# Branch A's output gates finished in the group's head, queries swapped by transfers, residual gate with moving columns, four probability buffers

## Chip, cores and metric

One core of a Trainium2 chip. The metric is the device time of one execution in microseconds (us); lower is better. The engines are named as in the profile: PE (matmul), PEld (its weight loads), DVE, ACT, POOL, and SP, whose queue issues every transfer of this kernel.

## What is computed

One encoder layer over two groups ("prompt", "sample") of 1024 tokens and width 1024, with shared weights, all in float32.

```
mod = silu(c) @ w_ada + b_ada;  shift, scale, gate = split(mod, 3)
h = rms_norm(x, norm_g) * (1 + scale) + shift
qa, ka, va, za, qb, kb, vb, zb, ga, gb = split(h @ w_in)
oa = gqa_attention(rope(rms(qa)), rope(rms(ka)), va) * silu(za)     # 8 query heads of 64, 2 kv heads
ob = rms(diff_attention(rope(rms(qb)), rope(rms(kb)), vb, lam)) * (1 - lam_init) * silu(zb)  # 4 heads, 2 maps
merged = sigmoid(ga) * (oa @ w_proj_a) + sigmoid(gb) * (ob @ w_proj_b)
y = x + gate * (merged @ w_out)
```

## The kernel before

**Precision.** Most products are made of float32r parts: a high part (ACT copies it) and a low part (DVE or POOL subtracts), with three matmuls for a pair of split operands. Weights come in by `load_w` through the tag `st` (3 buffers) and are split at L177 (ACT) and L179 (POOL, or DVE where the engines are alone).

**Stages of a group.** (1) A *head*: keys and values of branch A (`kva_gen`) and half of its queries (`qa_gen`), woven with a few banks of `z_gen`. (2) Six phases of attention, `phase(0)` to `phase(4)` and a last one; in each, attention is woven with filler work on PE: projections still needed (`proj_tt`, L488) and `z_gen` (L667), which makes the gate inputs za, zb, ga, gb. (3) The merge (L940) and the output projection `out_gen` (L969). The second group's normalisation (`ht_gen`) runs beside the first group's output projection.

**z_gen.** There are 12 items of 4 banks; a bank is 24 matmuls of 512 columns. ACT copies a finished bank to the tile `ev` (L673), and a transfer parks it in device memory as `zd`. `Z_HEAD` says how many of the 48 banks go to the head, `Z_SHARE` how many to each phase, and the rest comes in the last phase. Before, `gated_gen` reads a parked bank back in the last phase, applies Silu (L895), and multiplies the attention output by it.

**rms.** Each projected tile of tokens goes through ACT (copy L500, square L501), DVE (sum L504), POOL (L505: scale and epsilon; L506: power −0.5), and a rotation on POOL or DVE (L508 to L528). PE then transposes it (L539), and ACT and DVE split it (L541, L542). In a head, the engine of the rotation alternates by tile, and tile *t* is transposed after tile *t*+2 was projected (`LAG`).

**Attention.** A unit is 256 queries (two tiles of 128) of one head. A query tile holds its high part in one half of the partitions and its low part in the other; scores need it a second time with the halves exchanged. `swapped` makes that copy, `sw`, on POOL (L565), a tile of 128 queries at a time. Scores are four matmuls (L697, L698) into one of two PSUM banks `s`; DVE takes the negated maximum (L699); ACT takes the exponential (L700) into a tile `p` of the pool `ppool` (3 buffers). `flip` then transposes in 32×32 blocks on DVE (L734), and four transfers (L739) put `p` into `q`, from where the values are multiplied (L759, L760 in branch A, L799 in branch B). In branch B there are two maps for each query tile, joined on DVE (L733). A `p` buffer comes free when its transfers have landed.

**Order.** `weave` interleaves the streams by the shares in the tables (`ATT_W`, `IN_A`, `Z_A`, `LAST_ATT`, `LAST_FILL` and so on), attention is emitted at high priority, and a scheduler then sets each engine's order from its own estimate of times. Each engine and SP's queue run their instructions strictly in that order.

**The residual's gate.** `gate_gen` runs once, for both groups, in the first group's last phase. Before, the weights are the stationary operand and the moving one, `cT`, has 2 columns (L435), 64 matmuls that run as 128 instructions.

Of the kernel before, what the change touches and what calls it, by code (L numbers as in the profile page):

```python
# [48 lines left out]
    (0.1, 0.05, 0.45, 0.1, 0.15, 0.55),  # L49
)  # L50
Z_A = (
    (0.15, 0.0, 0.2, -0.1, 0.0, 0.0),
    (0.15, 0.05, 0.35, 0.05, 0.0, -0.1),
)
LAST_ATT, LAST_FILL = (44, 32)
GATED_A = -0.1
TAIL = 6
TAIL_A = 0.3
LAG = 2

# [28 lines left out]
def kernel(ctx: ExitStack, tc: tile.TileContext, t: dict):  # L89
# [336 lines left out]
    def gate_gen():  # L426
        for n in range(NCH):
            ps = gbank()[:, :2]
            for q in range(2):
                st = spool.tile([P, 4, P], F32, tag="st", name=nm("st"))  # L430
                col = 2 * D + n * P
                dma(st, w_ada[q * 512 : (q + 1) * 512, col : col + P].rearrange("(c p) n -> p c n", p=P))
                for c in range(4):
                    k = q * 4 + c
                    nc.tensor.matmul(ps, st[:, c], cT[:, k], start=(k == 0), stop=(k == NCH - 1))  # L435
            nc.vector.tensor_scalar(out=gatec[:, n], in0=ps, scalar1=bcol[:, 2, n : n + 1], scalar2=None, op0=ALU.add)
            yield 1
# [58 lines left out]
    def rms(ps, nh, e):  # L496
        n = nh * HD
        row = rtile()
        raw, sq = row[:, :n], row[:, 256 : 256 + n]
        nc.scalar.activation(raw, ps, AF.Copy)  # L500
        nc.scalar.activation(sq, raw, AF.Square)  # L501
        ss = tiny.tile([P, 4], F32, tag="ss", name=nm("ss"))[:, :nh]
        rs = tiny.tile([P, 4], F32, tag="rs", name=nm("rs"))[:, :nh]
        nc.vector.tensor_reduce(out=ss, in_=sq.rearrange("p (h d) -> p h d", d=HD), axis=AX.X, op=ALU.add)  # L504
        nc.gpsimd.tensor_scalar(out=ss, in0=ss, scalar1=1.0 / HD, scalar2=EPS, op0=ALU.mult, op1=ALU.add)  # L505
# [52 lines left out]
    def swapped(u, qt):  # L558

        qs = u["q"]  # L560
        sw = mtile("sw", [P, 2, P], F32R)[:, : len(qs)]
        sl = slice(qt * P, (qt + 1) * P)
        for m, q in enumerate(qs):
            for a, b in ((LO, HI), (HI, LO)):
                nc.gpsimd.tensor_scalar(  # L565
                    out=sw[a, m], in0=q[b, sl].bitcast(F32), scalar1=1.0, scalar2=1.0, op0=ALU.mult, op1=ALU.mult
                )
        return sw

# [26 lines left out]
    def qa_gen(st, half):  # L596
# [12 lines left out]
        def back(tt, x3):  # L609
            sl = slice(tt * P, (tt + 1) * P)  # L610
            pairs_T(x3, qs[0][:, :, sl], qs[1][:, :, sl])

        yield from pipelined(ht, w, front, back)

    def qkb_gen(ht, out, h):
# [40 lines left out]
    def z_gen(ht, col, dst, i0):  # L656
        w = load_w(w_cols(w_in, (col, 256)))
        for hf in range(2):
            for e in range(2):
# [13 lines left out]
                nc.scalar.activation(ev, ps, AF.Copy)  # L673
# [31 lines left out]
    def scores(u, i):  # L705
# [4 lines left out]
        if m == 0:  # L710
            u["sw"] = u["next"] if "next" in u else swapped(u, qt)
        pt = ptile()
        su = u["su"][:, qt : qt + 1] if m == 0 else tiny.tile([P, 1], F32, tag="su", name=nm("su"))
        softmax_unit(u["q"][m][:, qt * P : (qt + 1) * P], u["sw"][:, m], u["k"][m], pt, su)
        if m == 0:
            u[t] = [pt]
            u.pop("next", None)
# [114 lines left out]
    def attention(units):  # L832
# [3 lines left out]
        for n, (ph, make) in enumerate(units):  # L836
# [7 lines left out]
        for at, ph, n, i, qk in steps:  # L844
# [4 lines left out]
            with tc.high_priority(offset=AHEAD):  # L849
# [12 lines left out]
                if t is not None:  # L862
                    late.append(lambda u=live[n], t=t: flip(u, t))
                    if t == 0:
                        late.append(lambda u=live[n]: u.update(next=swapped(u, u["pr"] * 2 + 1)))
                    elif n + 1 < len(units) and units[n + 1][0] == ph:
                        live[n + 1] = units[n + 1][1]()
                        late.append(lambda u=live[n + 1]: u.update(next=swapped(u, u["pr"] * 2)))
# [5 lines left out]
    def gated_gen(st, i, hf, oT):  # L874
# [15 lines left out]
        for c in range(2):  # L890
# [4 lines left out]
            nc.scalar.activation(z, z, AF.Silu)  # L895
# [109 lines left out]
    def units_of(st):  # L1005
# [17 lines left out]

        units = []
        for half in range(2):
            units += [(half, lambda a=(half, i, pr): a_unit(*a)) for i in (0, 2, 1, 3) for pr in range(4)]
        for h in range(4):
            units += [(2 + h, lambda a=(h, pr): b_unit(*a)) for pr in range(4)]
# [9 lines left out]
    def z_item(st, i):  # L1038
        ht = st["ht"]
        if i < 2:  # L1040
            return z_gen(ht, C_ZA + i * 256, st["zd"], i * 2)
        if i < 4:
            return z_gen(ht, C_ZB + (i - 2) * 256, st["zd"], i * 2)
# [118 lines left out]
```

## Time and profile before

| | |
|---|---|
| runs | 2009.33, 2014.87, 2015.93 us; median 2014.87 |
| the profiled execution | 2017.56 us, span 2015.8 us, mean granted PE clock 0.974 |
| busy share | PE 95%, PEld 82%, DVE 65%, ACT 51%, POOL 48% |
| transfers | 278 MB, all large ones on one queue, 46.2% of the 16 DMA engines' span |

PE is busy nearly throughout, so time can be lost on it in two ways that the share does not show apart: short waits, and stretches in which its clock is granted at half. A window of the trace tells both: its length less PE's busy time, and the column of the granted clock.

### The profile page before, as it was taken

What the parts mean: (1) busy time and instruction counts of PE and PEld (TensorE: products, weight loads), DVE (VectorE), ACT (ScalarE), POOL (GpSimd) and SP (SyncE); (2) the same over time, 40 slices, a digit from 0 to 9 for tenths busy, and PEclk for the clock granted to TensorE, in tenths of its full rate; (3) what the DMA queues carried; (4) which work ended last, traced back from release to release, by engine and by line L of the source; (5) the groups of instructions that cost most, each with busy time, mean ns of one, the idle gap of its engine ahead of it and who ended that gap; (6) DMA issues with size and microseconds to landing.
All of it is one profiled execution on the core that took longest, in us unless ns stands there. A gap on an engine that the chain in (4) does not pass through costs nothing.

```text
span 2015.8 us, 31269 instructions
## 1 busy us (share of the span) xinstructions
PE 1924.6 (95%) x10554; PEld 1650.9 (82%) x10554; DVE 1305.9 (65%) x1798; ACT 1029.6 (51%) x1956; POOL 963.1 (48%) x1640
## 2 busy tenths in 40 slices
PE   8889999999999999889998899999999999998999
PEld 3778888888978988768888787888887888876887
DVE  4557766776787476546464778667777746664741
ACT  4445655565554345754323556566665434587420
POOL 2475723564677471331235675246577837522210
PEclk9999999999999996999998899999999999999999
DMA  8124545555443327754650345464544323565531
GB/s 306 48 71 109 147 139 137 148 150 154 109 125 95 90 81 206 223 191 160 208 188 32 99 123 152 137 169 126 157 127 126 88 74 90 160 212 192 183 119 73
DMA packets 255199, 278.35 MB, mean 138 GB/s; under 512 B 31680, under 2 KB 205888, under 8 KB 255040
## 3 DMA queue, kind: packets, MB, share of 16 engines
q1 hardware_dynamic: 255040, 276.36, 46.2%
q8 instruction: 84, 1.38, 0.3%
q14 instruction: 75, 0.61, 0.1%
HBM read 133.59 MB, written 42.01 MB: 87 GB/s over the span
## 4 chain that ended last, share of the span: by engine, by line
PE 58%; DVE 10%; DMA 10%; POOL 7%; ACT 6%; issue 5%; SPq 3%; ACTq 0%; POOLq 0%; DVEq 0%
PE f L667 15%; PE f L488 14%; PE f L969 4%; PE s L697 4%; PE s L698 4%; PE s L969 3%; DMA q<-p 3%; PE a L799 3%; DMA p<-zd 2%; PE a L759 2%; PE a L760 2%; SPq L739 2%; DVE m L699 2%; PE f L940 2%; ACT p L700 2%
## 5 line engine op out<-in xcount | busy, mean ns | idle before, releaser
L667 PE MATMUL f<-u,w 128*128 128x512 f32 x2208 | 580.6, 399 | 0.0
L488 PE MATMUL f<-w,u 128*128 128x256 f32 x3456 | 492.2, 288 | 2.8 <-ACT row L500 1.6
L488 PEld LDWEIGHTS f<-w,u 128*128 128x128 f32 x3456 | 464.1, 193 | 24.0 <-ACT row L500 2.7
L667 PEld LDWEIGHTS f<-u,w 128*128 128x128 f32 x2208 | 405.1, 191 | 76.0 <-ACT w L177 0.5
L700 ACT ACTIVATE p<-s,m 128x1024 f32<-128x1024 f32 x256 | 284.7, 1112 | 247.0 <-DMA q<-p 124.6
L699 DVE TENSOR_REDUCE m<-s 128x1 f32<-128x1024 f32 x256 | 310.3, 1217 | 71.6 <-PE s L698 68.2
L179 POOL TENSOR_TENSOR w<-st,w 128x512 fp32r<-128x512 f32 x168 | 231.9, 1396 | 238.7 <-ACT w L177 172.1
L565 POOL TENSOR_SCALAR sw<-u 64x128 fp32r<-64x128 f32 x520 | 180.4, 347 | 307.6 <-PE s L698 264.5
L734 DVE STREAM_TRANSPOSE p<-p 128x1024 f32<-128x1024 f32 x192 | 238.2, 1241 | 114.5 <-ACT p L700 109.2
L748 DVE TENSOR_TENSOR q<-q,hi 128x512 fp32r<-128x512 f32 x256 | 197.4, 790 | 55.0 <-ACT hi L747 53.0
L698 PE MATMUL s<-u,sw 128*128 128x512 f32 x512 | 209.1, 409 | 0.0
L747 ACT ACTIVATE hi<-q 128x512 fp32r<-128x512 f32 x256 | 153.5, 625 | 92.0 <-DMA q<-p 50.0
L177 ACT ACTIVATE w<-st 128x512 fp32r<-128x512 f32 x196 | 113.9, 625 | 93.9 <-DMA st<-in_w_in_dram 39.2
L940 PE MATMUL f<-u,w 128*128 128x512 f32 x564 | 143.5, 405 | 14.3 <-ACT ev L673 7.6
L940 PEld LDWEIGHTS f<-u,w 128*128 128x128 f32 x564 | 107.4, 193 | 39.6 <-DVE u L951 9.2
L759 PE MATMUL a<-hi,u 128*128 128x256 f32 x512 | 131.4, 283 | 5.0 <-DVE oo L776 5.0
L799 PE MATMUL a<-q,u 128*128 128x256 f32 x512 | 132.4, 395 | 1.4 <-issue 1.2
L760 PE MATMUL a<-q,u 128*128 128x256 f32 x512 | 128.6, 285 | 0.6 <-DVE q L748 0.6
L697 PE MATMUL s<-u 128*128 128x512 f32 x256 | 112.4, 440 | 16.5 <-ACT p L700 16.2
L506 POOL TENSOR_TENSOR rs<-ss,nhalf 128x4 f32<-128x4 f32 (+1 forms) x112 | 111.9, 999 | 7.4
L733 DVE SCALAR_TENSOR_TENSOR p<-p,r,p 128x1024 f32<-128x1024 f32 x64 | 91.8, 1434 | 35.2 <-POOL r L721 33.2
L697 PE MATMUL s<-u,u 128*128 128x512 f32 x256 | 104.6, 408 | 10.0 <-ACT p L700 9.7
(176 smaller groups left out, 2713.8 us busy)
## 6 DMA issues: line engine op xcount, KB each, us to landing
q<-p SPq DMA_DIRECT2D x768, 128.0 KB, 2.6
st<-in_w_in_dram SPq DMA_DIRECT2D x132, 256.0 KB, 3.1
zd<-ev SPq DMA_DIRECT2D x96, 256.0 KB, 2.4
p<-zd SPq DMA_DIRECT2D x64, 256.0 KB, 3.1
u<-in_w_ada_dram SPq DMA_DIRECT2D x8, 1024.0 KB, 10.4
st<-in_w_in_dram SPq DMA_DIRECT2D x64, 128.0 KB, 3.1
st<-in_w_out_dram SPq DMA_DIRECT2D x32, 256.0 KB, 3.0
row<-od SPq DMA_DIRECT2D x24, 256.0 KB, 3.3
```

The source lines that it names most:

```text
L179: e.tensor_tensor(out=wl, in0=st, in1=wh.bitcast(F32), op=ALU.subtract)
L488: nc.tensor.matmul(ps, lt[c][:, sl], w[:, c, wi, :], start=(k == 0), stop=(k == 23))
L565: nc.gpsimd.tensor_scalar(out=sw[a, m], in0=q[b, sl].bitcast(F32), scalar1=1.0, scalar2=1.0, op0=ALU.mult, op1=ALU.mult)
L667: nc.tensor.matmul(ps, w[:, c, wi, e * P : (e + 1) * P], rt[c], start=(k == 0), stop=(k == 23),)
L697: nc.tensor.matmul(s[:, sl], q, k[:, sl], start=True, stop=False)
L698: nc.tensor.matmul(s[:, sl], sw, k[:, sl], start=False, stop=True)
L699: nc.vector.tensor_reduce(out=m, in_=s, axis=AX.X, op=ALU.max, negate=True)
L700: nc.scalar.activation(pt.rearrange("p (j c a) -> p j c a", j=4, c=8), s.rearrange("p (c a j) -> p j c a", c=8, j=4), AF.Exp, bias=m, accu ...
L734: nc.vector.transpose(pt, pt)
L748: nc.vector.tensor_tensor(out=tl, in0=tl.bitcast(F32), in1=th.bitcast(F32), op=ALU.subtract)
L799: nc.tensor.matmul(acc, u["v"][:, k], pT[:, k], start=(k == 0), stop=(k == 7))
L940: nc.tensor.matmul(ps, w[:, c, wi, d * P : (d + 1) * P], o[:, oi, :], start=(k == 0), stop=(k == 11))
```

## The change

1. `z_gen` finishes branch A's gates: for the first two items (`SILU = 2`, 8 banks) L673's successor applies Silu instead of Copy, and `gated_gen` leaves Silu out for them. `Z_HEAD` grows from 5 and 3 banks to 8 and 6; the shares of the phases shrink, the group's sum staying at 47 banks in the first and rising from 46 to 47 in the second. The places and weights in the tables are set anew.
2. `swapped` copies the whole unit (256 queries) by two transfers (four in branch B) instead of four (eight) instructions of POOL. It is asked for when the first tile of the unit before has had its scores, across phases too where the queries are already made (`made`, `there`).
3. `gate_gen` makes the 2-row `cT` stationary and moves 512 columns of weights: 16 matmuls (32 instructions), a copy of the row, 8 transposes, 2 additions.
4. `ppool` has 4 buffers, `upool` 15 instead of 16; `sw` is twice as wide.
5. In `rms` the factor 1/64 goes into ACT's square, and the addition of epsilon goes from POOL to DVE.

```
-Z_SHARE = ((7, 20, 5, 3, 2, 5), (7, 18, 4, 3, 5, 6))
+Z_SHARE = ((7, 17, 5, 3, 3, 4), (9, 14, 7, 3, 2, 6))
-Z_HEAD = (5, 3);  Z_HEAD_A = (-0.35, -0.25)
+Z_HEAD = (8, 6);  Z_HEAD_A = (-0.4, -0.4)
-LAST_ATT, LAST_FILL = (44, 32);  GATED_A = -0.1
+LAST_ATT, LAST_FILL = (46, 30);  GATED_A = -0.3
...
+SILU = 2
-    upool = ent(tc.tile_pool(name="upool", bufs=16))
+    upool = ent(tc.tile_pool(name="upool", bufs=15))
-    ppool = ent(tc.tile_pool(name="ppool", bufs=3))
+    ppool = ent(tc.tile_pool(name="ppool", bufs=4))
...
     def gate_gen():
-        for n in range(NCH):
-            ps = gbank()[:, :2]
-            for q in range(2):
-                st = spool.tile([P, 4, P], F32, tag="st", name=nm("st"))
...
-                    nc.tensor.matmul(ps, st[:, c], cT[:, k], start=(k == 0), stop=(k == NCH - 1))
+        for half in range(2):
+            acc = gbank()[:2]
+            for k in range(NCH):
+                st = spool.tile([P, 512], F32, tag="st", name=nm("st"))
+                col = 2 * D + half * 512
+                dma(st, w_ada[k * P : (k + 1) * P, col : col + 512])
+                nc.tensor.matmul(acc, cT[:, k], st, start=(k == 0), stop=(k == NCH - 1))
+                if k % 2:
+                    yield 1
+            row = rtile()[:2]
+            nc.vector.tensor_copy(row, acc)
+            ps = gbank()[:, :8].rearrange("p (c g) -> p c g", g=2)
+            for c in range(4):
+                nc.tensor.transpose(ps[:, c, :], row[:, c * P : (c + 1) * P], ident[:2, :2])
...
     def rms(ps, nh, e):
-        nc.scalar.activation(sq, raw, AF.Square)
+        nc.scalar.activation(sq, raw, AF.Square, scale=1.0 / math.sqrt(HD))
...
-        nc.gpsimd.tensor_scalar(out=ss, in0=ss, scalar1=1.0 / HD, scalar2=EPS, op0=ALU.mult, op1=ALU.add)
+        nc.vector.tensor_scalar(out=ss, in0=ss, scalar1=EPS, scalar2=None, op0=ALU.add)
...
-    def swapped(u, qt):
+    def swapped(u):
-        sw = mtile("sw", [P, 2, P], F32R)[:, : len(qs)]
-        sl = slice(qt * P, (qt + 1) * P)
+        sw = mtile("sw", [P, 2, 256], F32R)[:, : len(qs)]
+        sl = slice(u["pr"] * 256, u["pr"] * 256 + 256)
         for m, q in enumerate(qs):
             for a, b in ((LO, HI), (HI, LO)):
-                nc.gpsimd.tensor_scalar(
-                    out=sw[a, m], in0=q[b, sl].bitcast(F32), scalar1=1.0, scalar2=1.0, op0=ALU.mult, op1=ALU.mult
-                )
+                dma(sw[a, m].bitcast(F32), q[b, sl].bitcast(F32))
...
     def z_gen(ht, col, dst, i0, fn=AF.Copy):
-                nc.scalar.activation(ev, ps, AF.Copy)
+                nc.scalar.activation(ev, ps, fn)
...
     def gated_gen(st, i, hf, oT):
-            nc.scalar.activation(z, z, AF.Silu)
+            if i >= SILU:
+                nc.scalar.activation(z, z, AF.Silu)
```

**How the engines' orders move.** Lines of the changed kernel lie up to 12 higher (L667 becomes L679, L697 and L698 become L709 and L710, L700 becomes L712, L799 becomes L810, L895 becomes L905, L931 becomes L941).

PE, last phase of the first group, where the residual's gate begins; `f` is the gate's PSUM bank, `st` its weights, `s` a bank of scores. Before:

```order
L539 MATMUL f_8230<-ident,row_8124 128x128
L435 MATMUL f_8314<-cT,st_8315 128x2 x4
L435 MATMUL f_8314<-cT,st_8321 128x2 x4
L435 MATMUL f_8333<-cT,st_8334 128x2 x4
L697 MATMUL s_8307<-u_7503 128x512
L698 MATMUL s_8307<-u_7503,sw_8300 128x512
L435 MATMUL f_8333<-cT,st_8340 128x2 x4
```

Now:

```order
L435 MATMUL f_8181<-st_8182,cT 2x512
L435 MATMUL f_8181<-st_8185,cT 2x512
L435 MATMUL f_8181<-st_8193,cT 2x512
L709 MATMUL s_8174<-u_7366 128x512
L710 MATMUL s_8174<-u_7366,sw_8104 128x512
L810 MATMUL a_8234<-q_8099,u_6905 128x256 x8
```

Between two score matmuls now stand a few long matmuls of 512 columns where many of 2 columns stood.

PE, end of the second group's head: the last transposes and the first scores. Before:

```order
L539 MATMUL f_11341<-ident,row_11222 128x128 x2
L539 MATMUL s_11348<-ident,row_11269 128x128 x2
L697 MATMUL s_11511<-u_10496,u_10945 128x512
L698 MATMUL s_11511<-u_10496,sw_11506 128x512
L697 MATMUL s_11511<-u_10496,u_10945 128x512
L698 MATMUL s_11511<-u_10496,sw_11506 128x512
L697 MATMUL s_11523<-u_10496,u_10945 128x512
```

Now:

```order
L709 MATMUL s_11371<-u_10260,u_10709 128x512
L710 MATMUL s_11371<-u_10260,sw_11366 128x512
L709 MATMUL s_11371<-u_10260,u_10709 128x512
L710 MATMUL s_11371<-u_10260,sw_11366 128x512
L679 MATMUL s_11220<-u_9904,w_11174 128x512
L679 MATMUL s_11220<-u_9906,w_11174 128x512
L679 MATMUL s_11220<-u_9904,w_11174 128x512 x2
L679 MATMUL s_11220<-u_9906,w_11174 128x512
L679 MATMUL s_11220<-u_9904,w_11174 128x512
L709 MATMUL s_11380<-u_10260,u_10709 128x512
```

Matmuls of z now stand between the first tiles' scores; the head's three more banks are spread over its last two thirds, and its first eight tiles (keys and values) have hardly any.

ACT, last phase of the second group: `p` beside `su` is an exponential, `row` at L895 a Silu of `gated_gen`, `p` at L931 a sigmoid of the merge. Before:

```order
L700 ACT_TABLE_LOAD
L700 ACTIVATE p_18842,su_18843<-s_18845,m_18844 128x1024
L895 ACT_TABLE_LOAD
L895 ACTIVATE row_18798<-row_18798 128x512
L700 ACT_TABLE_LOAD
L700 ACTIVATE p_18901,suB_138<-s_18903,m_18902 128x1024
```

Now:

```order
L941 ACT_TABLE_LOAD
L941 ACTIVATE p_18572<-p_18572 128x1024
L921 ACTIVATE u_18457<-row_18458 128x512
L222 ACTIVATE w_18765<-st_18774 128x512
L222 ACTIVATE w_18765<-st_18778 128x512
L921 ACTIVATE u_18457<-row_18469 128x512
L712 ACT_TABLE_LOAD
```

The exchange of tables at every exponential gives way to stretches with none. In the two last phases and merges together ACT's order holds 55 table loads before and 26 now; in the heads and first phases 1 before and 12 now; 58 and 40 in all.

More of the change, by code (lines that the diff above doesn't have):

```diff
@@ L426, in gate_gen @@
     def gate_gen():
-        for n in range(NCH):
-            ps = gbank()[:, :2]
-            for q in range(2):
-                st = spool.tile([P, 4, P], F32, tag="st", name=nm("st"))
[L431 to L437, printed above, removed]
+        for half in range(2):
[12 more added lines that the diff above has]
+                nc.tensor.transpose(ps[:, c, :], row[:, c * P : (c + 1) * P], ident[:2, :2])
+            cs = slice(half * 4, half * 4 + 4)
+            nc.vector.tensor_tensor(
+                out=gatec[:, cs], in0=ps, in1=bcol[:, 2, cs].unsqueeze(2).to_broadcast([P, 4, 2]), op=ALU.add
+            )
     def ht_gen(g, ht):
@@ L611, in back @@
             pairs_T(x3, qs[0][:, :, sl], qs[1][:, :, sl])
+            made[id(qs)] = tt + 1
         yield from pipelined(ht, w, front, back)
@@ L653, in vb_gen, with z_gen @@
             yield 1
-    def z_gen(ht, col, dst, i0):
+    def z_gen(ht, col, dst, i0, fn=AF.Copy):
         w = load_w(w_cols(w_in, (col, 256)))
@@ L835, in attention @@
         steps = []
-        for n, (ph, make) in enumerate(units):
+        for n, (ph, _, _) in enumerate(units):
             na, nv = (2, 4 + PV_LAG) if ph < 2 else (4, 5 + PV_LAG)
@@ L863, in attention @@
                     late.append(lambda u=live[n], t=t: flip(u, t))
-                    if t == 0:
-                        late.append(lambda u=live[n]: u.update(next=swapped(u, u["pr"] * 2 + 1)))
-                    elif n + 1 < len(units) and units[n + 1][0] == ph:
+                    if t == (0 if ph < 2 else 0) and n + 1 < len(units) and units[n + 1][2]():
                         live[n + 1] = units[n + 1][1]()
-                        late.append(lambda u=live[n + 1]: u.update(next=swapped(u, u["pr"] * 2)))
+                        late.append(lambda u=live[n + 1]: u.update(sw=swapped(u)))
             yield None
@@ L1022, in b_unit, with there @@
             }
+        def there(kind, n, pr):
+            return made.get(id(st[kind].get(n)), 0) > 2 * pr + 1
         units = []
         for half in range(2):
-            units += [(half, lambda a=(half, i, pr): a_unit(*a)) for i in (0, 2, 1, 3) for pr in range(4)]
+            units += [
+                (half, lambda a=(half, i, pr): a_unit(*a), lambda a=("qa", half, pr): there(*a))
+                for i in (0, 2, 1, 3) for pr in range(4)
+            ]
         for h in range(4):
-            units += [(2 + h, lambda a=(h, pr): b_unit(*a)) for pr in range(4)]
+            units += [
+                (2 + h, lambda a=(h, pr): b_unit(*a), lambda a=("qkb", h, pr): there(*a)) for pr in range(4)
+            ]
         return units
@@ L1039, in z_item @@
         ht = st["ht"]
+        fn = AF.Silu if i < SILU else AF.Copy
         if i < 2:
-            return z_gen(ht, C_ZA + i * 256, st["zd"], i * 2)
+            return z_gen(ht, C_ZA + i * 256, st["zd"], i * 2, fn)
         if i < 4:
-            return z_gen(ht, C_ZB + (i - 2) * 256, st["zd"], i * 2)
+            return z_gen(ht, C_ZB + (i - 2) * 256, st["zd"], i * 2, fn)
         i -= 4
```

31 lines of the change are left out of this document (16 added, 15 removed).

## The prediction

> **What bounds the kernel now.** I read the page first: busy time, the clock's row, and the chain that ended last, by engine.
>
> ```profile
> PE 1924.6 (95%) x10554; PEld 1650.9 (82%) x10554; DVE 1305.9 (65%) x1798; ACT 1029.6 (51%) x1956; POOL 963.1 (48%) x1640
> PEclk9999999999999996999998899999999999999999
> PE 58%; DVE 10%; DMA 10%; POOL 7%; ACT 6%; issue 5%; SPq 3%; ACTq 0%; POOLq 0%; DVEq 0%
> ```
>
> PE is the bound, with 91.2 us idle (2015.8 − 1924.6). The clock's row has dips at about 750 us and 1050 to 1150 us. So I asked for windows by stage, with length and busy time of PE, PEld, DVE, ACT and POOL, then the granted clock, DMA share and GB/s.
>
> ```profile
> 50.00:150.00 100.00, 87.02 (x536) 77.91 (x537) 57.16 (x135) 43.31 (x112) 60.98 (x102) 0.93 0.19 58
> 800.00:900.00 100.00, 87.44 (x388) 70.43 (x387) 53.26 (x72) 67.52 (x91) 29.37 (x31) 0.96 0.65 207
> 1050.00:1150.00 100.00, 87.95 (x547) 78.47 (x546) 55.51 (x125) 38.62 (x103) 57.18 (x107) 0.90 0.21 62
> 1150.00:1500.00 350.00, 342.36 (x2037) 302.37 (x2037) 261.77 (x321) 209.32 (x417) 193.25 (x324) 1.00 0.52 143
> 1750.00:1850.00 100.00, 89.84 (x390) 72.30 (x388) 61.87 (x81) 74.40 (x100) 24.70 (x39) 0.97 0.62 195
> ```
>
> The two heads (50 to 150, 1050 to 1150) idle 13.0 and 12.1 us, the two last phases 12.6 and 10.2: half of all idle time in a fifth of the span. In between PE is 98% busy, and there only removed PE work helps.
>
> **The residual's gate.** Lines here are a window, a group, and PE's timeline (start, length, count).
>
> ```profile
> 754.00:803.00 49.00, 49.00 (x225) 43.47 (x226) 31.86 (x46) 24.48 (x36) 8.83 (x24) 0.69 0.67 195
> L435 PE MATMUL f<-cT,st 128*128 128x2 f32 x128 | 20.4, 289 | 0.0
> 769.71 2.51 PE L435 MATMUL f<-cT,st 128*128 128x2 f32 x22
> 774.94 3.41 PE L435 MATMUL f<-cT,st 128*128 128x2 f32 x16
> 29.83 10.46 PE L298 MATMUL f<-u,cT 128*2 128x512 f32 x24
> 0.00:50.00 50.00, 42.38 (x169) 17.10 (x169) 24.74 (x42) 23.63 (x39) 11.07 (x14) 0.99 0.88 308
> 40.22 0.41 PE L307 MATMUL f<-ident,p 2*128 2x2 f32 x4
> 1150.00:1200.00 50.00, 49.85 (x309) 44.57 (x309) 40.42 (x51) 31.26 (x66) 36.47 (x60) 1.00 0.48 133
> ```
>
> All 128 old instructions lie in this window. PE never idles in it, yet its clock is 0.69: a 2-column matmul costs 2.51/22 = 114 ns at full clock and 3.41/16 = 213 ns at half. At full clock the window holds 49.0 × 0.69 = 33.8 us of work, 14.6 of it the gate (128 × 0.114). The new gate is 32 × 10.46/24 = 13.9 us plus 8 transposes at 0.41/4, 0.8 in all. If the clock stays full, PE needs 33.8 − 14.6 + 14.7 = 33.9 us, a gain of 15. But DVE holds 31.9 us of work here, and its highest share in a 50 us window is 40.42/50 = 81%: at that share the softmax sets 31.9/0.81 = 39.3 us. I take −10, between that and a clock that doesn't recover (14.7/0.69 = 21.3 against 20.4: +1). Bounds: −15 and +1.
>
> That the clock recovers rests on the rows at 29.83 and 0.00: matmuls of the same form (2-row stationary, 512 columns) run at the start of the span, and the granted clock of those 50 us is 0.99. The Trainium skill, "TensorE: Matmul & The Clock Gate", section "What's actually happening", has the clock follow how busy PE has been; read by busy time this would predict no half clock in a window that is 49.00 of 49.00 busy, so nothing for a new shape to restore, and the sum would lack these 10 us. The measured 0.69 speaks against that reading.
>
> **More banks in the heads.** PE's timeline with the wait ahead of an instruction in brackets, and two windows around those waits.
>
> ```profile
> 134.36 0.44 PE L539 MATMUL s<-ident,row 128*128 128x128 f32 x2 [3.24 <-POOL row L528]
> 147.51 0.44 PE L539 MATMUL f<-ident,row 128*128 128x128 f32 x2 [3.55 <-POOL row L528]
> 1101.70 0.69 PE L539 MATMUL f<-ident,row 128*128 128x128 f32 x2 [2.97 <-POOL row L528]
> 1129.44 0.80 PE L697 MATMUL s<-u,u 128*128 128x512 f32 x1 [5.77 <-ACT p L700]
> 125.00:155.00 30.00, 22.90 (x112) 18.84 (x111) 17.07 (x27) 12.54 (x27) 21.84 (x33) 0.89 0.41 120
> 1095.00:1145.00 50.00, 40.53 (x219) 34.25 (x218) 30.99 (x54) 21.62 (x47) 33.27 (x59) 0.83 0.24 67
> 83.92 0.33 PE L539 MATMUL f<-ident,row 128*128 128x128 f32 x1 [1.67 <-POOL row L528]
> 93.41 0.30 PE L539 MATMUL f<-ident,row 128*128 128x128 f32 x1 [2.68 <-ACT u L541]
> 1126.89 1.28 ACT L700 ACT_TABLE_LOAD   x1
> ```
>
> The four waits, 15.5 us, stand where no z matmul does; six more banks stand there now, taken from phases that are full, so filled waits are gained whole. Half the clock's loss in the windows (30 × 0.11 + 50 × 0.17 = 11.8) gives 6 more. Against it, the second group's first eight tiles lose their fillers and look like the first's, with 1.67 + 2.68 us of waits: 4.4. And 11 more table loads beside the first exponentials (11 × 1.28 = 14 us of ACT) delay scores, which have two banks only; ACT is 60% busy in the window from 1150, so most of it is covered and I charge 4 us. Sum −13. Bounds: all idle and clock of the windows, 7.1 + 9.5 + 11.8 = −28; and +6, if the new waits come and the old stay in part.
>
> **Fewer table loads at the end.** Groups, and waits of PE in the last phases.
>
> ```profile
> L895 ACT ACT_TABLE_LOAD x26 | 33.4, 1283 | 21.3 <-DMA row<-zd 20.9
> L895 ACT ACTIVATE row<-row 128x512 f32<-128x512 f32 x24 | 15.2, 632 | 0.9 <-DMA row<-zd 0.6
> 815.14 0.50 PE L697 MATMUL s<-u 128*128 128x512 f32 x1 [2.01 <-ACT p L700]
> 851.27 2.78 PE L940 MATMUL f<-u,w 128*128 128x512 f32 x6 [2.23 <-ACT ev L673]
> 1824.81 3.67 PE L940 MATMUL f<-u,w 128*128 128x512 f32 x9 [4.31 <-ACT ev L673]
> 869.20 3.01 PE L940 MATMUL f<-u,w 128*128 128x512 f32 x12 [2.43 <-DVE u L951]
> ```
>
> 29 loads (37 us) and 16 Silu (16 × 0.63 = 10 us) leave ACT in two stages in which it is busy for 142 us; the Silu return as the activation of `ev`, in place of the Copy, at no cost of their own. PE idles 22.7 us there; the three waits shown behind ACT make 8.6, and 7 us go to the clock (100 × 0.04 + 100 × 0.03). Waits behind DVE stay (869.20). I take −11, between 8.6 and the two together, nearer the first. Bounds: −25 and 0. `upool` with one buffer less can delay the merge's tiles in this stage; that is why 0 is the bound.
>
> **Buffers of probabilities, swapped queries, epsilon.** Groups, a wait total (us, times, longest), and one line's DMA issues on SP (ns: least, median, most).
>
> ```profile
> L697 PE MATMUL s<-u 128*128 128x512 f32 x256 | 112.4, 440 | 16.5 <-ACT p L700 16.2
> L697 PE MATMUL s<-u,u 128*128 128x512 f32 x256 | 104.6, 408 | 10.0 <-ACT p L700 9.7
> ACT p L700 <- DMA q<-p: 124.6, 66, 5.7
> L565 POOL TENSOR_SCALAR sw<-u 64x128 fp32r<-64x128 f32 x520 | 180.4, 347 | 307.6 <-PE s L698 264.5
> L505 POOL TENSOR_SCALAR ss<-ss 128x4 f32<-128x4 f32 x96 | 26.2, 273 | 124.7 <-DVE ss L504 120.5 <-DVE ssB L823 0.4
> L823 DVE COPY ssB<-f 128x2 f32<-128x2 f32 x32 | 4.9, 153 | 17.0 <-PE f L821 16.8
> L739 SPq DMA_DIRECT2D q<-p x768: 542/602/1926, 147.3 to 1851.8; - x192
> od<-oo SPq DMA_DIRECT2D x64, 64.0 KB, 2.1
> ```
>
> ACT waits 125 us for a free `p`; PE feels 26.5 us of late exponentials, 18.7 without the 5.77 and 2.01 above. A fourth buffer takes that reason away, but the maximum on DVE remains behind it: −6, a third. Bounds: −19 and +5. POOL loses 180 us and 256 transfers appear on SP: 256 × 0.602 = 154 us of its queue, over some 1400 us of attention. SP's order has a unit's `sw` ahead of the flips of the unit three before, some 35 us early (a group's 32 units of branch A take about 400 us), against 2.1 us for a landing of that size; I cost it at nothing while that lead lasts. The 112 additions move from POOL (273 ns) to DVE (some 150 ns, a small copy's row): 17 us of DVE, hidden behind PE.
>
> **The sum.** −10 − 13 − 11 − 6 = −40 against the profiled execution's 2017.56: 1978. That execution is 2.7 us above the median of the three runs (2014.87), so in the runs' terms the gain is 37 us, 1.8%. A difference under 0.3% (6 us) can't be told from none.
>
> **Rivals.**
> - *Only the gate pays* (chance 0.17). The order is new throughout; waits that close here open elsewhere, as the waits at 83.92 and 93.41 do. For it: the releasers in the waits quoted are POOL, ACT and DVE alike, so no one cause is removed. Against it: the named places have work in them now. Time 2017.6 − 10 = 2008, or down to 1992 with half of the rest.
> - *The clock stays low in the gate* (0.07). For it: PE alternates there with short score bursts. Against it: the rows at 29.83 and 0.00. Time 1978 + 10 = 1988.
> - *SP's queue turns into the bound: slower* (0.09). A `sw` transfer waits for its buffer, that is for the scores of two units before, and SP holds the flips and weights queued behind it. If a part of the 154 us is exposed, ACT and PE wait again for `p` and `st`. It eats the gain from 40/154 = 26% exposed, and is slower by over 0.3% from 46/154 = 30%; at half the time is 1978 + 77 = 2055. Against it: at 0.602 us, the 768 flips take 462 us of some 1400, so SP has room. The Trainium skill, "DMA: Bandwidth & Descriptors", "Rules for kernel authors", says that two transfers to disjoint partition halves serialize, since both use the same 16 DMA engines; by that a pair would land after 4.2 us rather than about 2.7, still far below the lead. No run here shows it yet.
> - *Nearly all idle time and clock go* (0.15). Two thirds of the bounds, 0.67 × (15 + 28 + 25 + 19) = 58: 1959 and below.
>
> The forecast itself, 1966 to 1991, has 0.50; no change at all 0.02. Faster by over 0.3%: 0.50 + 0.07 + 0.15 + 0.14 of the first rival = 0.86; within: 0.05; slower: 0.09. The range for 8 in 10, 1956 to 2008, leaves out the tail of the last case below and the slower case above.
>
> **What would show it.** Gate: the granted clock near 1.0 while L435 runs, about 40 us for its stretch, DVE ahead of PE's waits. Heads: no waits above 2 us at the last transposes and first scores; new ones in the second group's first eight tiles. End: ACT below 60 us busy in the last 100 us of each attention, and waits of PE behind DVE only. Buffers: ACT's wait for `q<-p` well below 125 us. I am wrong if PE's idle sum stays near 91 us, if the half clock moves elsewhere, or if SP's waits for PE ahead of `sw` grow long.

## Result and the profile after

The changed kernel takes 1980.04 us in the median of four runs (1978.85 to 1981.89), against 2013.81 for the kernel before on the same chip: ratio 0.9836, 95% interval 0.9817 to 0.9855, so 1.6% faster. Its profiled execution took 1980.88 us, span 1979.1; the span before was 2015.8. Two executions below, 2671.01 us of the kernel with the old gate and 4813.19 us of the one with one weight moved, were slow ones and are left out of all medians.

The page of the changed kernel, its line of busy time:

```profile
PE 1905.0 (96%) x10466; PEld 1623.3 (82%) x10466; DVE 1323.4 (67%) x1908; ACT 992.4 (50%) x1922; POOL 755.0 (38%) x1006
```

PE idles 74.1 us (1979.1 − 1905.0) instead of 91.2. The mean granted clock of the span went from 0.974 to 0.983; the missing share times the span is 53 us before and 34 us now. Idle time gives 17 us and the clock 19, together 36, and the span is 36.7 us shorter. The gain is lost PE time that came back.

Where it came back, by stage. First the kernel before, then the changed one, windows cut where about the same work begins and ends: first head, first attention, residual gate, last phase and merge; then second head, second attention, last phase and merge. Columns: length, busy time of PE, PEld, DVE, ACT and POOL (with instructions), granted clock, DMA share, GB/s.

```profile
50.00:152.00 102.00, 89.02 (x541) 79.48 (x542) 58.31 (x136) 43.31 (x112) 60.98 (x102) 0.92 0.19 59
152.00:754.00 602.00, 586.30 (x3472) 518.19 (x3470) 429.96 (x541) 327.88 (x661) 350.06 (x637) 0.99 0.45 124
754.00:802.40 48.40, 48.40 (x223) 42.96 (x224) 31.86 (x46) 23.88 (x36) 8.23 (x24) 0.68 0.68 197
802.40:959.00 156.60, 144.04 (x637) 117.20 (x638) 92.29 (x127) 90.94 (x123) 40.86 (x39) 0.98 0.60 193
1048.00:1132.00 84.00, 72.69 (x485) 67.26 (x484) 41.88 (x110) 30.12 (x88) 51.51 (x92) 0.91 0.16 51
1132.00:1784.00 652.00, 633.03 (x3671) 555.88 (x3671) 464.64 (x587) 364.05 (x716) 373.90 (x677) 0.99 0.46 130
1784.00:1924.00 140.00, 132.75 (x589) 107.89 (x590) 84.17 (x117) 87.49 (x116) 32.44 (x34) 0.98 0.58 191
```

```profile
50.00:156.00 106.00, 100.93 (x610) 90.24 (x611) 58.75 (x153) 47.90 (x118) 53.99 (x75) 0.95 0.22 69
156.00:756.70 600.70, 581.33 (x3430) 512.99 (x3429) 439.31 (x581) 325.90 (x661) 263.45 (x374) 0.98 0.49 136
756.70:792.80 36.10, 33.83 (x118) 16.12 (x118) 25.97 (x33) 13.51 (x27) 1.36 (x4) 1.00 0.62 187
792.80:940.00 147.20, 140.14 (x628) 115.10 (x629) 98.27 (x137) 79.11 (x114) 38.71 (x32) 0.98 0.70 228
1028.00:1116.00 88.00, 81.64 (x534) 74.28 (x533) 45.34 (x128) 33.76 (x94) 51.87 (x74) 0.95 0.19 61
1116.00:1739.00 623.00, 613.59 (x3608) 541.36 (x3607) 458.24 (x610) 351.76 (x700) 271.31 (x385) 1.00 0.51 142
1739.00:1888.00 149.00, 135.94 (x603) 111.28 (x602) 100.99 (x140) 80.25 (x112) 29.23 (x26) 0.95 0.62 203
```

Take each window's idle time (length less PE) plus its clock loss. For the loss I use half of the time that the trace shows at half clock, which is finer than the rounded column:

| stage | idle + clock loss before, us | after, us | difference | predicted |
|---|---|---|---|---|
| both heads | 13.0 + 8.2, 11.3 + 7.4 = 39.9 | 5.1 + 4.9, 6.4 + 4.3 = 20.7 | −19 | −13 |
| residual gate | 0.0 + 15.4 = 15.4 | 2.3 + 0.0 = 2.3 | −13 | −10 |
| attention, first group | 15.7 + 6.8 = 22.5 | 19.4 + 10.2 = 29.6 | +7 | } −6 |
| attention, second group | 19.0 + 8.2 = 27.2 | 9.4 + 2.5 = 11.9 | −15 | } |
| last phases | 12.6 + 3.4, 7.3 + 3.2 = 26.5 | 7.1 + 3.4, 13.1 + 6.8 = 30.4 | +4 | −11 |

The differences add up to −36. So the sum came out nearly as predicted (−40), but not by its terms: three gave somewhat more, and one lost a little where a gain was forecast.

One border is uncertain. Before, a wait of PE lies just ahead of the second group's last phase as cut here:

```profile
1783.72 0.79 PE L697 MATMUL s<-u 128*128 128x512 f32 x1 [3.50 <-ACT p L700]
```

The changed kernel's last window holds 35 score matmuls, and as many stand in the window of before if that begins at 1769.6 instead of 1784. With that border the last phases differ by 0 instead of +4, and the second attention by −12 instead of −15. The sum stays.

**The gate**, PE's timeline and its window:

```profile
756.69 2.74 PE L435 MATMUL f<-st,cT 128*2 128x512 f32 x6
...
779.71 1.02 PE L435 MATMUL f<-st,cT 128*2 128x512 f32 x2 [1.68 <-DMA st<-in_w_ada_dram]
```

2.74/6 is 457 ns for one matmul, and PE is granted its full clock throughout (1.00 above, 0.68 before). What is late next is the weights: 1.68 us of the 2.3 us that PE idles here.

**The heads.** The window at the first group's last transposes, which was 22.90 busy at clock 0.89, and the largest wait left in either head:

```profile
125.00:155.00 30.00, 29.80 (x164) 25.30 (x163) 16.65 (x34) 14.04 (x31) 16.61 (x21) 1.00 0.34 101
1113.33 0.79 PE L709 MATMUL s<-u,u 128*128 128x512 f32 x1 [4.58 <-ACT p L712]
```

The waits of 3 us behind POOL's rotated rows are gone; the only other wait over 2 us in a head is one of 2.32 at 77.24, behind ACT's `ev`. The one at the second group's first scores shrank only from 5.77 to 4.58 us.

**The last phases.** PE's waits over 3.5 us there, then DVE's timeline ahead of the largest, and ACT's ahead of that:

```profile
839.17 5.06 PE L950 MATMUL f<-u,w 128*128 128x512 f32 x11 [3.82 <-ACT ev L685]
1792.29 1.01 PE L832 MATMUL f<-ones_c,at 128*128 128x1 f32 x4 [4.13 <-DVE u L961]
1798.20 5.49 PE L950 MATMUL f<-u,w 128*128 128x512 f32 x12 [4.90 <-DVE u L961]
1794.85 0.16 DVE L731 RECIPROCAL r<-su 128x1 f32<-128x1 f32 x1 [1.82 <-ACT p L712]
1795.49 1.28 DVE L744 SCALAR_TENSOR_TENSOR p<-p,r,p 128x1024 f32<-128x1024 f32 x1 [0.48 <-POOL r L732]
1796.79 0.75 DVE L916 SCALAR_TENSOR_TENSOR row<-row,subg,row 128x512 f32<-128x512 f32 x1
1797.46 0.68 DVE L961 TENSOR_TENSOR u<-f,p 128x512 f32<-128x512 f32 x1
1792.32 1.28 ACT L712 ACT_TABLE_LOAD   x1
1793.61 1.11 ACT L712 ACTIVATE p<-s,m 128x1024 f32<-128x1024 f32 x1
```

PE waits for L961, a product of the merge, until 1798.20. It stands on DVE behind the join of two maps of branch B, and that in turn waits for an exponential of ACT. So the order of DVE holds PE, and behind it still stands ACT: a table load of 1.28 us runs right ahead of that exponential. Of the 55 loads in the last phases and merges 26 are left, 13 of them for the merge's sigmoids.

Added over the two windows (before with the border at 1769.6), PE's waits behind ACT fell from 15.6 to 5.5 us. Those behind DVE grew from 7.7 to 11.5, waits of 2.9 behind POOL and transfers are new, and the clock's loss grew from 6.8 to 10.2.

**The attentions.** PE's waits for exponentials in the changed kernel; before they were 16.2 and 9.7 us:

```profile
L709 PE MATMUL s<-u 128*128 128x512 f32 x256 | 109.0, 426 | 11.0 <-ACT p L712 8.9 <-DMA q<-p 2.0
L709 PE MATMUL s<-u,u 128*128 128x512 f32 x256 | 103.4, 404 | 8.3 <-ACT p L712 8.2
```

The rest of what the two attentions lost and gained (+7 and −15) was not followed to a cause.

### The profile page after: what moved, and what is told of

It is laid out like the page before. It is cut to its first block, busy times and chain, and to the rows that moved or that the text cites. A ratio compares the mean times of both kernels' runs of the same rounds, so it can differ in the third digit from the quotient of the medians.

```text
span 1979.1 us, 30627 instructions
## 1 busy us (share of the span) xinstructions
PE 1905.0 (96%) x10466; PEld 1623.3 (82%) x10466; DVE 1323.4 (67%) x1908; ACT 992.4 (50%) x1922; POOL 755.0 (38%) x1006
## 4 chain that ended last, share of the span: by engine, by line
PE 58%; DVE 9%; DMA 8%; issue 5%; SPq 5%; ACT 5%; POOL 2%; ACTq 0%; DVEq 0%; POOLq 0%
PE f L679 14%; PE f L497 13%; PE f L979 5%; PE f L950 4%; PE a L810 4%; PE s L979 4%; DMA q<-p 4%; PE s L709 4%; PE s L710 3%; SPq L750 3%; DVE m L711 2%; DVE q L759 2%; PE s L950 2%; PE a L771 2%; PE a L770 2%
## 5 line engine op out<-in xcount | busy, mean ns | idle before, releaser
L679 PE MATMUL f<-u,w 128*128 128x512 f32 x2232 | 578.6, 398 | 5.1 <-ACT w L179 3.0
L497 PEld LDWEIGHTS f<-w,u 128*128 128x128 f32 x3456 | 457.8, 192 | 27.7 <-ACT ev L685 6.1
L679 PEld LDWEIGHTS f<-u,w 128*128 128x128 f32 x2232 | 409.2, 190 | 85.6 <-ACT w L179 4.2
L712 ACT ACTIVATE p<-s,m 128x1024 f32<-128x1024 f32 x256 | 284.5, 1111 | 275.9 <-DVE m L711 153.4
L710 PE MATMUL s<-u,sw 128*128 128x512 f32 x512 | 203.5, 398 | 0.0
L771 PE MATMUL a<-q,u 128*128 128x256 f32 x512 | 130.5, 288 | 1.8 <-DVE q L759 1.7
L810 PE MATMUL a<-q,u 128*128 128x256 f32 x512 | 125.7, 382 | 1.8 <-DMA q<-p 1.8
L709 PE MATMUL s<-u 128*128 128x512 f32 x256 | 109.0, 426 | 11.0 <-ACT p L712 8.9
L709 PE MATMUL s<-u,u 128*128 128x512 f32 x256 | 103.4, 404 | 8.3 <-ACT p L712 8.2
L710 PEld LDWEIGHTS s<-u,sw 128*128 128x128 f32 x512 | 97.3, 190 | 15.8
L810 PEld LDWEIGHTS a<-q,u 128*128 128x128 f32 x512 | 95.1, 192 | 16.1 <-DMA q<-p 2.1
```

The costliest lines, as they stand in the source:

```text
L497: nc.tensor.matmul(ps, lt[c][:, sl], w[:, c, wi, :], start=(k == 0), stop=(k == 23))
L679: nc.tensor.matmul(ps, w[:, c, wi, e * P : (e + 1) * P], rt[c], start=(k == 0), stop=(k == 23),)
L709: nc.tensor.matmul(s[:, sl], q, k[:, sl], start=True, stop=False)
L710: nc.tensor.matmul(s[:, sl], sw, k[:, sl], start=False, stop=True)
L712: nc.scalar.activation(pt.rearrange("p (j c a) -> p j c a", j=4, c=8), s.rearrange("p (c a j) -> p j c a", c=8, j=4), AF.Exp, bias=m, accu ...
L810: nc.tensor.matmul(acc, u["v"][:, k], pT[:, k], start=(k == 0), stop=(k == 7))
```

## Experiments

Parts tried alone on the kernel before, and parts taken out of the changed kernel. Ratios are to the kernel before, run on the same chip. Another run of the changed kernel (below) gave 0.9828.

**The new gate alone**, in the kernel before:

```
     def gate_gen():
-        (weights stationary, cT moving: 128 matmuls of 2 columns)
+        (cT stationary, 512 columns of weights moving: 32 matmuls, a copy, 8 transposes, 2 additions)
```

> The kernel before with the new residual gate alone (cT stationary, 512 columns moving). Theory A, the granted clock fell to 0.69 because 2-column matmuls hardly use the array: the clock is about 1.0 while the gate runs, its stretch of 49 us shrinks to 34 to 39 us, and the time falls by 10 to 15 us, to about 2000. Theory B, the clock follows PE's busy time and the low clock in that stretch has another cause: the clock stays near 0.69 there and the time is within 3 us of before.

Measured: 2029.05 us against 2023.14, ratio 1.0032 (1.0012 to 1.0052). Windows of this kernel: the gate, the second group's attention (nothing was edited there), and the worst part of that.

```profile
754.00:796.00 42.00, 35.47 (x117) 15.93 (x115) 30.16 (x39) 19.58 (x31) 8.97 (x23) 0.96 0.69 206
1130.00:1790.00 660.00, 626.94 (x3601) 550.72 (x3600) 474.17 (x587) 363.61 (x712) 367.78 (x672) 0.98 0.46 128
1480.00:1580.00 100.00, 84.56 (x439) 72.70 (x438) 82.76 (x103) 54.01 (x107) 58.47 (x116) 0.91 0.44 118
```

The gate's stretch shortened from 48.4 to 42 us with its clock back at 0.96. But PE idles 33 us in the second attention, 14 more than before. The scheduler set every engine's order anew after the edit, and the new order has gaps there; 15 us of them stand in the window from 1480. The local gain is shown, and so is that it need not reach the end. In the old order it is 7 us (idle time and clock loss 8.2 instead of 15.4), not the 13 of the table.

**The old gate in the changed kernel** (the same edit backwards).

> The changed kernel with the old residual gate (2 columns moving). Theory A: stretches of half clock come back in the gate, about 30 us of them, and the time rises by 10 to 15 us over the changed kernel's 1980, to 1990 to 1995. Theory B, in the changed order the softmax sets the pace of that stretch and the gate's form no longer counts: within 4 us of 1980.

Measured: 1998.52 us, ratio 0.9873 (0.9835 to 0.9912), so some 0.4% (7 us) above the changed kernel, with intervals that overlap. A window and two pieces of PE's timeline, from this kernel:

```profile
750.00:800.00 50.00, 48.84 (x248) 42.84 (x247) 31.88 (x49) 15.93 (x31) 9.73 (x21) 0.83 0.55 153
780.31 3.41 PE L437 MATMUL f<-cT,st 128*128 128x2 f32 x16
787.13 2.88 PE L437 MATMUL f<-cT,st 128*128 128x2 f32 x24
```

The clock falls to 0.83 with PE 98% busy, and the 2-column matmul takes 213 ns (3.41/16) in one place and 120 (2.88/24) in another. With the form goes the clock, and its loss of 8.5 us in this window is of the size of the difference. The Trainium skill, "TensorE: Matmul & The Clock Gate", "What's actually happening", says that the gate follows how busy PE has been. If busy means the time that the profile calls busy, this run and the kernel before disagree with it; what the hardware counts instead, none of these runs can tell.

**The heads' banks alone**, in the kernel before:

```
-Z_SHARE = ((7, 20, 5, 3, 2, 5), (7, 18, 4, 3, 5, 6));  Z_HEAD = (5, 3);  Z_HEAD_A = (-0.35, -0.25)
+Z_SHARE = ((7, 17, 5, 3, 2, 5), (7, 15, 4, 3, 5, 6));  Z_HEAD = (8, 6);  Z_HEAD_A = (-0.4, -0.4)
```

> The kernel before with three more z banks in each head (8 and 6 instead of 5 and 3, taken from the second phase) and the later offsets of the heads, nothing else; Silu stays at the end. Theory A, the banks fill PE's waits in the heads: the idle time of the two heads falls from 25 us to about 12, with some 6 us less lost to the clock, and the time falls by 13 to 20 us. Theory B, the heads gained through the shorter rms chain and POOL's freedom, not through the banks: less than 6 us.

Measured: 2042.44 us, ratio 1.0088 (1.0058 to 1.0118). The two attentions of this kernel:

```profile
159.00:771.00 612.00, 584.74 (x3421) 514.37 (x3419) 434.29 (x541) 326.52 (x660) 349.91 (x637) 0.97 0.44 121
1170.00:1813.00 643.00, 610.67 (x3530) 535.39 (x3529) 463.34 (x583) 356.83 (x705) 360.81 (x661) 0.98 0.46 127
```

The heads, in windows of their own, idle 8.1 and 4.8 us instead of 13.0 and 11.3, and their clock loss is 7.1 us instead of 15.6, so the banks do fill the waits: −20 us in the heads, as much as in the whole change. The attentions idle 27 and 32 instead of 16 and 19, at a lower clock. Again the stage gains and the whole loses.

**How much does a change of the order alone move?** In the changed kernel, one weight of the weave:

```
-    (1.07, 0.837, 1.1, 0.95, 1.07, 1.52),
+    (1.07, 0.837, 1.12, 0.95, 1.07, 1.52),
```

> The changed kernel with one weight of the order's table moved from 1.10 to 1.12, to see what a new order alone does. If the named causes carry the change, the time stays within 4 us of the changed kernel. If any new order shifts waits by chance, it moves by 5 to 10 us either way, and single differences of that size in the other runs mean nothing.

Measured: 1984.44 us, ratio 0.9816 (0.9774 to 0.9858): no difference from the changed kernel. The edit left nearly the whole order of PE in place (10443 of its 10466 matmuls stand where they stood), so it bounds the cost of a small shift, not that of an order made anew.

**The changed kernel again**, beside the next three on one chip.

> The changed kernel itself, so that the next three stand beside it on the same chip. Expected by every theory: its ratio to the kernel before again at 0.984, within 0.003.

Measured: 1981.11 us, ratio 0.9828 (0.9792 to 0.9864). PE idles 10.7 us in the second group's last phases here and 13.1 in the first profile; the idle time of every other stage agrees within about 1 us. The three kernels that follow are compared with this one.

**Silu back in the last phases** (of the changed kernel):

```
-SILU = 2
+SILU = 0
```

> The changed kernel with branch A's Silu back in the last phase, everything else as it is. Theory A, the table loads there delayed PE: ACT's busy time in the two last phases rises by some 15 to 20 us each, PE's waits behind ACT come back, and the time rises by 8 to 15 us. Theory B, the change's last phases lose as much (13.1 us of idle PE in the second) as before although ACT has less to do, because the waits behind DVE that stand next in line set the time: within 4 us of the changed kernel.

Measured: 1988.07 us, ratio 0.9857 (0.9828 to 0.9887): 7 us above the repeated run in the median, with intervals that overlap. The loads of that line in the changed kernel and in this one, then a window of the second group's last phases in each:

```profile
L905 ACT ACT_TABLE_LOAD x9 | 11.5, 1283 | 0.2
1740.00:1840.00 100.00, 86.94 (x383) 70.61 (x383) 63.85 (x89) 59.12 (x80) 19.69 (x20) 0.93 0.71 232
```

```profile
L905 ACT ACT_TABLE_LOAD x22 | 28.2, 1283 | 21.6 <-DMA row<-zd 21.4
1740.00:1840.00 100.00, 84.82 (x356) 67.95 (x355) 63.69 (x87) 77.61 (x102) 20.83 (x21) 0.91 0.71 225
```

With Silu late, ACT is 77.61 us busy in those 100 us, and both last phases are longer (152.5 and 157.0 us against 146.9 and 147.5 of the repeated run, in the profiled executions, of which this kernel's was its slowest, 1995.47 us). PE's waits behind ACT there are 13.2 us, against 5.5 in the changed kernel's profile and 3.5 in the repeated run's. So the place and the kind of loss are those of the first theory; the time lies between the two theories, about 7 us by the medians, near the 8.6 us of waits that the prediction started from. It doesn't show in the table of stages, since the changed order has new waits at the same place.

**The gates where they stood before** (in the changed kernel, earlier among the attention):

```
-GATED_A = -0.3
+GATED_A = -0.1
```

> The changed kernel with the gates of the last phase at their old offset (-0.1 instead of -0.3). In the changed kernel's second group PE waits 4.1 and 4.9 us for DVE in the merge, with the gates of branch A just ahead on DVE. Theory A, the gates come too late there: the two waits go and the time falls by 5 to 9 us. Theory B, the offset trades these waits for waits of the softmax earlier: within 4 us.

Measured: 1993.31 us, ratio 0.9871 (0.9845 to 0.9897), 12 us above the repeated run. The loss is not where the gates are consumed but where they begin. The stretch of the residual gate (35.6 us long in the repeated run, 25.84 of them busy on DVE), and the largest wait in it:

```profile
760.10:801.80 41.70, 36.81 (x123) 17.23 (x122) 30.35 (x41) 15.96 (x31) 1.71 (x5) 0.96 0.71 202
782.87 1.02 PE L435 MATMUL f<-st,cT 128*2 128x512 f32 x2 [2.03 <-DMA st<-in_w_ada_dram]
```

Six us go there: DVE has 4.5 us more to do, 4 of them for the gates (L910, L920, L922). That the transfers of the gates also compete with the weights of the residual gate is likely, but not shown apart. In the second group's merge the two waits behind L961 are not gone but others, of 3.01 and 3.02 us, so neither theory holds. Another 5 us of idle time lie in the second attention, whose cause I did not follow.

**Three buffers of probabilities** (in the changed kernel):

```
-    ppool = ent(tc.tile_pool(name="ppool", bufs=4))
+    ppool = ent(tc.tile_pool(name="ppool", bufs=3))
```

> The changed kernel with 3 probability buffers instead of 4. Theory A, the fourth buffer is worth what was predicted or more: ACT's wait for the transfers of p rises from 106 us to 150 us or more, the attention phases lose 6 to 15 us. Theory B, the maximum on DVE stands right behind: the wait moves from one releaser to the other and the time stays within 4 us.

Measured: 2005.46 us, ratio 0.9934 (0.9911 to 0.9956), 24 us above the repeated run. Waits (total, times, longest) of ACT and of SP, in the changed kernel and in this one:

```profile
ACT p L712 <- DMA q<-p: 106.3, 51, 5.9
SPq L574 <- PE s L710: 27.3, 13, 6.8
```

```profile
ACT p L712 <- DMA q<-p: 128.5, 55, 5.8
SPq L574 <- PE s L710: 87.0, 41, 7.1
```

ACT waits for a free `p` only 22 us longer. The larger difference is on SP: its queue stands 87 us, not 27, at a `sw` transfer whose buffer PE is still reading, with the flips behind it. On PE, the idle time behind exponentials (L709) is 22.2 us, against 16.1 in the repeated run: 6 us, which is what the prediction gave the buffer. Where the other 18 us come from is open. The order is largely a new one here (6694 of PE's 10466 matmuls stand where they stood), and a new order cost 13 us and more in the runs with one part alone. The wait at `sw` suggests the rival "SP's queue turns into the bound" in a milder form, which the fourth buffer holds off; it is not shown that it carries the 18 us.

**Swaps on POOL again** (in the changed kernel, a whole unit at a time):

```
-                dma(sw[a, m].bitcast(F32), q[b, sl].bitcast(F32))
+                nc.gpsimd.tensor_scalar(out=sw[a, m], in0=q[b, sl].bitcast(F32), scalar1=1.0, scalar2=1.0, op0=ALU.mult, op1=ALU.mult)
```

> The changed kernel, but the swapped copy of a whole unit of queries is made by POOL (256 columns an instruction) in place of transfers; asked for as early as before. Theory A (the transfers themselves carry a part of the gain, since POOL has other work behind the copies): POOL gets some 256 instructions of about 0.5 us back, 130 us; waits of PE behind POOL's rows return in the heads, and the time is 5 to 15 us above the changed kernel, ratio to the kernel before 0.985 to 0.993. Theory B (what matters is that the copy is asked for early, and POOL has room): within 4 us of the changed kernel, 0.981 to 0.985; ACT's wait for q<-p falls below 106 us, since SP has 154 us less to issue.

Measured: 1993.62 us (1983.94 to 2006.3), ratio 0.9886 (0.9843 to 0.9929). POOL has 118.5 us of swaps. The time falls in the first theory's range, but the interval overlaps that of the repeated run (0.9792 to 0.9864), and the place is not the one named: the heads idle 7.6 and 6.7 us, hardly more than 5.1 and 6.4. PE idles 22 and 16 us in the attentions instead of 19 and 9 (in the profiled execution, the slowest of the four). That ACT would wait less for `q<-p` with a lighter queue on SP was wrong as well (116.1 us). So the transfers are worth 0 to 20 us, and why is open; the order of the engines is new here too.

**Twice as many swaps on SP** (in the changed kernel, the same bytes):

```
-                dma(sw[a, m].bitcast(F32), q[b, sl].bitcast(F32))
+                for x in range(2):
+                    y = slice(x * 128, x * 128 + 128)
+                    dma(sw[a, m, y].bitcast(F32), q[b, sl][:, y].bitcast(F32))
```

> The changed kernel, but each transfer of the swapped queries is split in two of 128 columns: 256 more issues on SP, some 154 us of its queue, of the same bytes. Theory A (the lead of the copies hides SP's issue time, as the prediction has it): within 5 us of the changed kernel, ratio 0.981 to 0.986. Theory B (SP's queue is near its bound, the fourth rival of the prediction, and its doubled cost would show): 10 to 40 us above the changed kernel, ratio 0.988 to 1.003, and ACT's wait for q<-p above 125 us.

Measured: 2045.72 us, ratio 1.0144 (1.0121 to 1.0166), 61 us above the changed kernel (0.9836 × 2017.49 = 1984.4), more than either theory gave. One window of the second attention in the changed kernel, then here, where three rows of SP's queue and POOL's wait follow.

```profile
1330.00:1430.00 100.00, 99.52 (x597) 87.69 (x596) 77.28 (x106) 62.90 (x128) 47.85 (x69) 1.00 0.57 159
```

```profile
1330.00:1430.00 100.00, 76.80 (x387) 63.48 (x387) 72.22 (x87) 55.23 (x102) 11.01 (x8) 0.88 0.55 144
1411.42 0.54 SPq L793 DMA_DIRECT2D od<-oo  x1
1412.31 2.55 SPq L752 DMA_DIRECT2D q<-p  x4
1414.90 1.66 SPq L203 DMA_DIRECT2D st<-in_w_in_dram  x3
POOL w L181 <- ACT w L179: 119.7, 5, 63.0
```

SP issues almost without a pause, at 0.6 us a transfer, while the DMA engines stay 55% busy: they are not the limit. Between 1350 and 1414.90 the queue issues flips, outputs and swaps, and no weights. ACT splits the next weights as soon as they land, and POOL, which follows ACT, has waited 63.0 us. PE has 141 filler matmuls in the window instead of 383; attention alone can't keep it busy, and its clock falls to 0.88. Added over the trace, SP's issue instructions take 807 us before, 981 in the changed kernel and 1134 here. In the densest 100 us of each that is about 60, 71 and 88 us. The first step went with a gain, the second with a loss of 61 us. The second theory's sign did not come: ACT's wait for `q<-p` fell to 84.2 us, instead of rising above 125. What PE lacks in this window is filler work. That SP issues the weights so late is the scheduler's order, made anew for the longer queue; how much of the 61 us is the queue itself, the run doesn't separate.

**The tables of before with the code of the changed kernel**, and **the tables of the changed kernel with the code of before**: all of `Z_SHARE`, `Z_HEAD`, `Z_HEAD_A`, `ATT_W`, the places, `LAST_ATT`, `LAST_FILL` and `GATED_A` exchanged.

> The changed kernel's code (gate form, swaps by transfer, four buffers, Silu moved, rms) with the tables of the kernel before: 5 and 3 banks in the heads, the old shares, weights and places. Theory A (the named mechanisms carry the gain whatever the order): ratio 0.985 to 0.992, the clock full in the gate's stretch, the heads' waits as before. Theory B (the retuned order carries most, and code in an order that wasn't made for it opens waits elsewhere, as in the runs with one part alone): ratio 0.995 to 1.01.

> The code of the kernel before with the tables of the changed one: 8 and 6 banks in the heads, the new shares, weights and places; gate, swaps, three buffers, Silu and rms as before. Theory A (the tables gain only with the code beside them): ratio 0.997 to 1.012, the heads' idle time and half clock small, the gain lost in the attention's stretches, and waits of ACT for q<-p of 120 us or more. Theory B (the banks in the heads pay by themselves, 13 to 19 us): ratio 0.990 to 0.994.

Measured: the new code with the old tables 2009.48 us, ratio 0.9952 (0.9933 to 0.9971); the old code with the new tables 2038.76 us, ratio 1.0103 (1.0079 to 1.0128). Windows: the second attention of the first of these, then of the other.

```profile
1139.00:1771.00 632.00, 610.33 (x3531) 537.42 (x3531) 466.45 (x618) 352.48 (x696) 262.95 (x370) 0.98 0.52 143
```

```profile
1155.00:1800.00 645.00, 613.51 (x3541) 538.97 (x3540) 455.23 (x568) 344.20 (x696) 369.82 (x665) 0.98 0.45 123
```

By the ratios on 2017.49, the code alone gains 10 us, the tables alone lose 21, and both together gain 33: 44 us belong to neither alone. The second attention idles 22 us with the first kernel and 31 with the second, but 9 where code and tables fit each other. The time of the code-alone run lies where the second theory had it, by which the order carries most of the gain, though not in the form "the tables pay": they pay only with this code. Nor was the clock full in the gate's stretch of that run: 0.93 over 47 us, with 6.2 us of idle PE.

## Why the prediction was right, and where not

- **The gate: right, but half of the gain from elsewhere.** Predicted −10 with the clock near 1.0 and a stretch of about 40 us; measured −13, 1.00 and 36.1 us. The prediction had DVE as the next limit at 39.3 us. DVE holds only 25.97 us of work in the stretch, and PE's longest wait there is for weights. The softmax is the same (maxima, joins and transposes: 23.6 us before, 23.4 now); what left is 6.2 us for the gates of branch A (L900, L910, L912 before), which the new tables place later. With the gates where they were, the stretch is 41.7 us, and with the new form alone 42.0. So the form alone gave 7 of the 13 us, less than forecast, and the rest came with the later gates, which the prediction did not count. The rival by which the clock stays low is refuted, and the run with the old gate ties the clock to the form of the matmul.
- **The heads: the mechanism right, the size low.** −19 instead of −13. The waits behind POOL and the clock went as described, and the run with the banks alone gave the heads the same 20 us. The charge of 8 us for new waits (4.4 at the second group's first tiles, 4 for table loads) was the mis-sized term: the only new wait over 2 us is at 77.24 in the *first* head, and the second head kept its largest wait (4.58) for the very reason that was to cost more, an exponential that comes late.
- **Fewer table loads: the step that failed.** ACT fell below 60 us in the last phases (56.57 in the 100 us from 800, 59.12 from 1740), as described, and the moved Silu is worth about 7 us by the run without it. PE's waits behind ACT fell by 10 us (15.6 to 5.5), somewhat more than the 8.6 forecast. But the last phases came out between 0 and +4 us rather than at −11. The step assumed that waits behind ACT, once gone, are not replaced, and that the half clock goes with them. Waits behind DVE grew by 3.8 us (9.0 stand at L961, at 1792 and 1798, since DVE runs in order), 2.9 behind POOL and transfers are new, and the clock lost 3.4 more. "Waits behind DVE stay" was written, and that they could grow was not priced. Nor were the loads that stay: one stands in the chain to the wait at 1798, and one ahead of the ACT wait at 839, there after a wait of ACT for a parked gate.
- **Buffers and swaps: −6 held as a sum, and the wait it was made from moved by about as much.** ACT's wait for `q<-p` fell only from 124.6 to 106.3 us, so "well below 125" was weak; its wait for the maximum on DVE grew from 102.5 to 153.4, as "remains behind it" says. PE's idle time behind exponentials fell from 25.9 to 17.1 us, and with three buffers it is 6 us above the repeated run. But the two attentions gave +7 and −15 (−12 with the other border), and that wait alone explains neither of them. The kernel with three buffers is 24 us slower, four times the term, with SP's queue 60 us longer at `sw`. The prediction charged the swaps at nothing; that buffer and swaps depend on each other it did not price.
- **SP's queue: the rival didn't happen, but was nearer than its chance of 0.09 says.** The reason given against it, that SP has room, holds for 256 transfers of 0.59 us, and with 512 the kernel is 61 us slower. By the Trainium skill, "DMA: Bandwidth & Descriptors", "Rules for kernel authors", transfers to disjoint partition halves serialize, which gave an estimate of 4.2 us for a pair. Here each landed 2.1 us after its issue in the median (4.2 at most), so at 64 KB no run shows that cost.
- **The rival "only the gate pays" named the right danger.** "Waits that close here open elsewhere" is what the gate alone and the banks alone did, and it ended slower than the kernel before. The prediction had it as a partial loss in the change as a whole, where it was held off by an order that fitted the code. That the time came out 2 us from the forecast owes something to luck: terms off by −6, −3, −2 and +15 (by −6, −3, +1 and +11 with the other border).

## What to carry to other kernels

When a scheduler makes the whole order from an estimate, a part's gain in its own stage can be predicted from the trace, but not its gain in the end: price a new order as a term of its own, with both signs and some tens of us here, and retune the order before a part is judged. Before work is moved to a queue that issues in order, add up the queue's issue time in the *densest* 100 us, not over the span: with 88 us of issue there, weights stood behind small transfers and PE lacked filler work while the DMA engines were 55% busy. Removing the waits behind one engine is worth only the lead over what is next in line, so look up what stands ahead of the awaited instruction there.

## What the runs showed of the hardware

- PE's clock was granted at 0.68 in a stretch in which the profile shows it busy without a gap, under matmuls with a moving operand of 2 columns; with 512 moving columns and a stationary operand of only 2, it was 1.00 although PE idled 2.3 of 36.1 us. So the form that uses less of the array, but moves more columns, kept the clock; with more idle time beside it, its stretch had 0.96 (5 to 7 of 42 us idle) and 0.93 (6 of 47).
- A transfer within on-chip memory cost SP 0.59 us of issue time at 64 KB and no less at 32 KB. SP's issues of `sw` in the changed kernel and in the one with twice as many (ns: least, median, most):

```profile
L574 SPq DMA_DIRECT2D sw<-u x256: 461/591/1585, 121.0 to 1741.6; - x128
L576 SPq DMA_DIRECT2D sw<-u x512: 461/594/2027, 112.0 to 1805.3; - x171
```
